# Low parts of the retention projection weights: a negated ScalarE copy plus an adding transfer in place of a VectorE subtraction

## The chip, the cores and the metric

The kernel runs on one core of one Trainium2 chip. The metric is the device time of one execution in microseconds (us). A core has TensorE (PE; its weight loads are listed as PEld), VectorE (DVE), ScalarE (ACT), GpSimd (POOL) and SyncE (SP), each with its own instruction stream in program order; streams meet only at semaphores. On-chip memory has 128 partitions; a tile "128x768" is 128 partitions by 768 elements.

## What is computed

Two decoder layers on 256 tokens of width 1024, in float32. Cut to what matters:

```python
for l in range(2):
    x = x + 0.5 * swiglu(rms_norm(x), ffn1_wg, ffn1_wu, ffn1_wd)   # hidden width 2816
    z = rms_norm(x) @ w_in[l]       # cut into rq rk rv rg mq mk mv ca cg
    mix = [retention(rq, rk, rv, rg), moba_attention(mq, mk, mv), conv_module(ca, cg)]
    x = x + concat(mix) @ w_out[l]
    x = x + 0.5 * swiglu(rms_norm(x), ffn2_wg, ffn2_wu, ffn2_wd)
return rms_norm(x, final_norm)
```

Retention uses four projections of width 384 (rq, rk, rv, rg), the attention three (mq, mk, mv), the convolution two of width 256.

## The kernel before

Every float32 weight matrix is multiplied as a sum of two parts: a high part `whi` (the weight rounded by a ScalarE copy to the type float32r) and a low part `wlo` (weight minus high part). The product of an activation and a weight is then high by high, high by low and low by high: `mm3` (lines 201 to 203), where the activations are the stationary operand, and `mm2w` (207, 208), where the weights are.

Weights come as a stream of 172 units. `stream_setup` lists them in the order of use; a unit of `w_in` (384 columns wide, half of the 1024 rows) is 128x1536, the others 128x2048. `fetch` issues one load on SP's queue into a `raw` tile, of which there are three (`RBUFS`); so a load waits until every reader of the unit three places earlier is done. `pump` makes one piece, half a unit: a ScalarE copy of `raw` into `whi` (line 145) and a VectorE subtraction into `wlo` (line 146). Ten pieces can be alive (`WBUFS`). `take` hands pieces to the matmuls, `free` returns a place, and `tick`, called between groups of matmuls, pumps at most one piece and advances the chains of work that were spawned (rotary embedding, attention, convolution, retention).

The PE instructions stand in the order in which the code issues them; the other engines' instructions are ordered by a planner that simulates the program at build time, except in short stretches that are marked as ordered.

The mixing stage (`mix`) takes the pieces in this order: mq and mk (8 pieces), the convolution's two gates (4), mv (4), then rq, rk, rv, rg (4 each), then the output projection (8). `chunk(w, t, ...)` runs the 24 matmuls of one projection for 128 tokens; its pieces are freed while the second half of the tokens runs. Around the retention weights these chains run:
- `rope`: a ScalarE copy out of PSUM (line 510), three GpSimd instructions on 128x96 (516 to 518), and four ticks later three PE transposes (line 505) and a ScalarE copy.
- `moba_group`: score matmuls (558), a VectorE maximum `nm` (562), ScalarE exponentials (569), PE transposes (576), ScalarE copies (578), matmuls with the values (588).
- `rot`: two VectorE products (528, 529), one GpSimd addition on 128x384 (530), transposes six ticks later.
- `conv`: 62 VectorE instructions of a depthwise convolution (693, 695), given a low rank by the planner.

In the profiled execution the pieces of rq to rg are, in each mixing stage, the 16 executions of line 145 that follow those of mv; in the first one they start at 224.12 us and end at 265.73.

Of the kernel before, what the change touches and what calls it, by code (L numbers as in the profile page):

```python
# [11 lines left out]
F32 = mybir.dt.float32  # L12
# [3 lines left out]
AF = mybir.ActivationFunctionType  # L16
OP = mybir.AluOpType
# [37 lines left out]
class Kernel:  # L55
# [38 lines left out]
    def stream_setup(self):  # L94
        a = self.a
        u = []
        for l in range(L):
            for f in (2 * l, None, 2 * l + 1):
                if f is None:
                    u += [(a["win"][l, 0, h], 1536) for h in range(2)]  # L100
                    u += [(a["win"][l, 1, h], 1536) for h in range(2)]
                    u += [(a["wcv"][l, i], 2048) for i in range(2)]
                    u += [(a["win"][l, i, h], 1536) for i in range(2, 7) for h in range(2)]
                    u += [(a["wout"][l, i], 2048) for i in range(4)]
                    continue
                u += [(a["wga"][f, i], 2048) for i in range(2)]
                for p in range(1, FT // 2):
                    u += [(a["wgb"][f, 2 * p - 2 + i], 2048) for i in range(2)]
                    if p > 1:
                        u.append((a["wd"][f, p - 2], 2048))  # L110
                u += [(a["wd"][f, i], 2048) for i in range((FT - TAIL) // 2, FT // 2)]
        self.units = u
        self.raws = []
        self.npieces = 0
        self.live = 0
        self.ready = deque()
# [13 lines left out]
    def pump(self):  # L130
        nc = self.nc
        u, i = divmod(self.npieces, 2)
        if u == len(self.units) or self.live == WBUFS:
            return False
        while len(self.raws) < min(u + RBUFS, len(self.units)):
            self.fetch()
        raw, w = self.raws[u]
        hi = self.wp.tile([P, 1024], F32R, tag="whi", bufs=WBUFS, name=self.name("whi"))[:, :w]
        lo = self.wp.tile([P, 1024], F32R, tag="wlo", bufs=WBUFS, name=self.name("wlo"))[:, :w]
        parts = 2 if u < 2 else 1  # L140
        p = w // parts
        for j in range(parts):
            c = slice(j * p, (j + 1) * p)
            src = raw[:, i * w + j * p:i * w + (j + 1) * p]
            nc.scalar.activation(hi[:, c], src, AF.Copy)  # L145
            nc.vector.tensor_tensor(lo[:, c], src, hi[:, c].bitcast(F32), op=OP.subtract)  # L146
        self.ready.append((hi, lo))
        self.npieces += 1
        self.live += 1
        return True  # L150
# [834 lines left out]
```

## Time and profile before

| | before |
|---|---|
| median of 3 runs, us | 1001.3 (999.83 to 1002.02) |
| the profiled execution: time, us | 1000.19 |
| its span, first to last instruction, us | 998.4 |
| granted TensorE clock (mean) | 0.998 |
| PE busy | 981.6 us (98%) |
| DVE busy | 685.5 us (69%) |
| ACT busy | 537.9 us (54%) |
| POOL busy | 64.1 us (6%) |
| DMA, mean | 181 GB/s |

The profile tells for each engine how long it was busy, and for an idle stretch which other instruction ended it. A PE that is busy 98% of the span has 16.8 us without work in all. The first mixing stage runs from about 205 to 312 us, the second from about 694 to 802.

### The profile page before, as it was taken

The numbers are of one execution on the slowest core, as the hardware profiler recorded it, in microseconds if no ns is written. First come the engines' busy times: TensorE is split into PE (matmuls) and PEld (weight loads), VectorE is DVE, ScalarE is ACT, GpSimd is POOL, SyncE is SP. The second block draws the span as 40 slices with busy tenths as digits, with TensorE's granted clock in tenths as the row PEclk, the third lists the DMA queues.
The fourth block names the chain that finished last, engine by engine and source line by source line (L and its number), as shares of the span: only waits on it lengthen the run. The fifth ranks groups of instructions, "written<-read, shape, count | busy, mean of one in ns | idle before, by whom it ended". The sixth has DMA issues, their size and how long they took to land.

```text
span 998.4 us, 13763 instructions
## 1 busy us (share of the span) xinstructions
PE 981.6 (98%) x5312; PEld 847.6 (85%) x5312; DVE 685.5 (69%) x1032; ACT 537.9 (54%) x904; POOL 64.1 (6%) x109
## 2 busy tenths in 40 slices
PE   6999999999999999999999999999999999999997
PEld 5888888898998888888888888888989888888885
DVE  6886565569976866666576656566699677666653
ACT  6755555366554755555465545454665456555542
POOL 1000000021141000000000000002100400000000
PEclk9999999999999999999999999999999999999999
DMA  8955554336441855555546555544545347555511
GB/s 309 347 194 201 175 204 156 142 122 214 170 170 64 302 204 172 201 177 199 181 173 218 179 193 186 188 150 139 186 143 197 138 148 253 175 204 174 205 44 43
DMA packets 28722, 180.69 MB, mean 181 GB/s; under 512 B 3440, under 2 KB 3824, under 8 KB 10480
## 3 DMA queue, kind: packets, MB, share of 16 engines
q1 hardware_dynamic: 27360, 176.07, 50.7%
q10 hardware_dynamic: 1296, 3.74, 1.0%
q8 instruction: 42, 0.69, 0.3%
q14 instruction: 24, 0.20, 0.1%
HBM read 178.74 MB, written 1.05 MB: 180 GB/s over the span
## 4 chain that ended last, share of the span: by engine, by line
PE 90%; DVE 6%; DMA 1%; ACT 1%; issue 1%; SPq 0%; POOL 0%; POOLq 0%; ACTq 0%; DVEq 0%
PE tr L207 15%; PE mm L207 15%; PE acc L451 8%; PE acc L448 8%; PE acc L447 8%; PE tr L208 7%; PE mm L208 7%; PE mm L201 4%; PE mm L202 4%; PE mm L203 4%; DVE wlo L146 3%; DVE ac L695 2%; PE acc L207 1%; PE tr L354 1%; PE acc L638 1%
## 5 line engine op out<-in xcount | busy, mean ns | idle before, releaser
L146 DVE TENSOR_TENSOR wlo<-raw,whi 128x1024 fp32r<-128x1024 f32 (+2 forms) x348 | 403.3, 1171 | 184.1 <-ACT whi L145 180.3
L145 ACT ACTIVATE whi<-raw 128x1024 fp32r<-128x1024 f32 (+2 forms) x348 | 348.6, 1013 | 229.0 <-PE acc L451 92.3
L207 PE MATMUL tr<-hT,whi 128*128 128x512 f32 x640 | 228.0, 397 | 0.2 <-DVE hfl L197 0.2
L207 PE MATMUL mm<-hT,whi 128*128 128x512 f32 x640 | 227.3, 396 | 0.0
L208 PE MATMUL mm<-hT,wlo 128*128 128x256 f32 x640 | 178.7, 279 | 0.0
L208 PE MATMUL tr<-hT,wlo 128*128 128x256 f32 x640 | 178.7, 279 | 0.0
L207 PEld LDWEIGHTS tr<-hT,whi 128*128 128x128 f32 x640 | 120.2, 188 | 29.2 <-PE mm L208 0.4
L207 PEld LDWEIGHTS mm<-hT,whi 128*128 128x128 f32 x640 | 120.2, 188 | 28.5
L447 PE MATMUL acc<-whi,hfh 128*128 128x512 f32 x352 | 139.2, 395 | 0.0
L448 PE MATMUL acc<-wlo,hfh 128*128 128x512 f32 x352 | 138.7, 394 | 0.0
L208 PEld LDWEIGHTS mm<-hT,wlo 128*128 128x128 f32 x640 | 120.6, 189 | 1.5
L208 PEld LDWEIGHTS tr<-hT,wlo 128*128 128x128 f32 x640 | 120.7, 189 | 0.0
L451 PE MATMUL acc<-whi,hfl 128*128 128x512 f32 x352 | 115.8, 396 | 0.0
L201 PE MATMUL mm<-whi,hT 128*128 128x384 f32 (+1 forms) x288 | 106.7, 371 | 0.7 <-ACT hT L196 0.7
L203 PE MATMUL mm<-whi,hT 128*128 128x384 f32 (+1 forms) x288 | 101.2, 351 | 0.0
L202 PE MATMUL mm<-wlo,hT 128*128 128x384 f32 (+1 forms) x288 | 101.1, 351 | 0.0
L447 PEld LDWEIGHTS acc<-whi,hfh 128*128 128x128 f32 x352 | 66.5, 189 | 15.1
L451 PEld LDWEIGHTS acc<-whi,hfl 128*128 128x128 f32 x352 | 66.3, 188 | 15.2
L448 PEld LDWEIGHTS acc<-wlo,hfh 128*128 128x128 f32 x352 | 66.3, 188 | 13.7
L433 ACT ACTIVATE s<-part 128x256 f32<-128x256 f32 x80 | 33.2, 414 | 79.2 <-DVE part L213 79.1
L213 DVE TENSOR_TENSOR part<-part,tr 128x256 f32<-128x256 f32 x80 | 33.6, 420 | 47.1 <-ACT part L212 47.1
L201 PEld LDWEIGHTS mm<-whi,hT 128*128 128x128 f32 x288 | 54.7, 190 | 5.5 <-issue 1.3
(151 smaller groups left out, 954.2 us busy)
## 6 DMA issues: line engine op xcount, KB each, us to landing
raw<-in_wgb SPq DMA_DIRECT2D x80, 1024.0 KB, 4.9
raw<-in_wd SPq DMA_DIRECT2D x44, 1024.0 KB, 4.9
raw<-in_win SPq DMA_DIRECT2D x28, 768.0 KB, 4.6
raw<-in_wout SPq DMA_DIRECT2D x8, 1024.0 KB, 4.8
raw<-in_wga SPq DMA_DIRECT2D x6, 1024.0 KB, 5.3
raw<-in_wcv SPq DMA_DIRECT2D x4, 1024.0 KB, 4.8
raw<-in_wga SPq DMA_DIRECT2D x8, 256.0 KB, 6.9
g<-in_fgain ACTq DMA_DIRECT2D x3, 512.0 KB, 3.5
```

The costliest lines, as they stand in the source:

```text
L145: nc.scalar.activation(hi[:, c], src, AF.Copy)
L146: nc.vector.tensor_tensor(lo[:, c], src, hi[:, c].bitcast(F32), op=OP.subtract)
L201: mm(out, ah, wh, start=start, stop=False)
L202: mm(out, ah, wl, start=False, stop=False)
L203: mm(out, al, wh, start=False, stop=stop)
L207: mm(out, wh, x, start=start, stop=False)
L208: mm(out[:, :S], wl, x[:, 0], start=False, stop=stop)
L213: self.nc.vector.tensor_tensor(v, lo, ps[:, :S], op=OP.add)
L433: nc.scalar.activation(s, v, AF.Silu)
L447: mm(ys[t][h], hi[:, ts], wh[:, n], start=first, stop=False)
L448: mm(ys[t][h], hi[:, ts], wl[:, n], start=False, stop=False)
L451: mm(ys[t][h], lo[:, ts], wh[:, n], start=False, stop=last)
```

## The change

For the eight units of rq, rk, rv and rg in each layer (units 41 to 48 and 127 to 134 of the stream, counted from 0), which make 32 of the 348 executions of line 146, the subtraction is replaced by two steps: ScalarE writes the negated weight, rounded, into `wlo`, and a transfer that GpSimd issues adds the raw weight to it in place. The sum is the same low part. All other pieces keep the subtraction.

```diff
     def stream_setup(self):
         a = self.a
         u = []
+        self.added = set()
...
                     u += [(a["wcv"][l, i], 2048) for i in range(2)]
+                    self.added |= {len(u) + i for i in range(2, 10)}
                     u += [(a["win"][l, i, h], 1536) for i in range(2, 7) for h in range(2)]
...
             nc.scalar.activation(hi[:, c], src, AF.Copy)
-            nc.vector.tensor_tensor(lo[:, c], src, hi[:, c].bitcast(F32), op=OP.subtract)
+            if u in self.added:
+                nc.scalar.activation(lo, src, AF.Copy, scale=-1.0)
+                nc.gpsimd.dma_start(lo, src, accum_op=OP.add)
+            else:
+                nc.vector.tensor_tensor(lo[:, c], src, hi[:, c].bitcast(F32), op=OP.subtract)
```

## Rows read from the trace of the kernel before

**Rows 1.** The page's first part: busy us (share of the span) xinstructions.
```profile
PE 981.6 (98%) x5312; PEld 847.6 (85%) x5312; DVE 685.5 (69%) x1032; ACT 537.9 (54%) x904; POOL 64.1 (6%) x109
```
**Rows 2.** Busy time by stretch: stretch, its length, each engine, PE clock, DMA share, GB/s.
```profile
0.00:205.00 205.00, 196.27 (x1012) 166.75 (x1013) 139.97 (x226) 114.10 (x191) 8.30 (x27) 1.00 0.60 210
...
220.00:290.00 70.00, 69.59 (x467) 65.92 (x466) 67.24 (x122) 41.12 (x77) 8.96 (x13) 1.00 0.50 173
...
710.00:780.00 70.00, 69.59 (x468) 65.97 (x466) 67.34 (x122) 41.57 (x78) 9.27 (x13) 1.00 0.50 172
802.00:998.40 196.40, 189.55 (x984) 160.41 (x984) 118.41 (x167) 98.69 (x163) 3.20 (x9) 0.99 0.46 158
```
**Rows 3.** Waits of PE, whole span: us in total, times, longest us.
```profile
PE tr L354 <- DVE xr L348: 8.5, 3, 8.1
PE acc L588 <- ACT q L578: 0.8, 2, 0.4
```
**Rows 4.** Groups of instructions by shape: lines 146 and 145, 768 wide.
```profile
L146 DVE TENSOR_TENSOR wlo<-raw,whi 128x768 fp32r<-128x768 f32 x56 | 52.1, 950 | 13.4 <-ACT whi L145 13.4
...
L145 ACT ACTIVATE whi<-raw 128x768 fp32r<-128x768 f32 x56 | 46.2, 845 | 20.9 <-PE mm L203 9.4 <-PE acc L451 3.7 <-PE mm L207 3.2
```
**Rows 5.** Timeline of ACT, first mixing stage: start us, us, instruction [idle before, releaser].
```profile
224.12 0.85 ACT L145 ACTIVATE whi<-raw 128x768 fp32r<-128x768 f32 x1 [0.19 <-PE mm L203]
...
225.91 0.47 ACT L510 ACTIVATE w<-mm 128x384 f32<-128x384 f32 x1
...
235.21 0.85 ACT L145 ACTIVATE whi<-raw 128x768 fp32r<-128x768 f32 x1 [0.51 <-PE mm L203]
...
238.44 0.37 ACT L569 ACTIVATE q<-acc,nm 128x128 f32<-128x128 f32 x1 [1.08 <-DVE nm L562]
...
240.41 0.22 ACT L569 ACTIVATION_READ_ACCUMULATOR q<-acc,nm 128x1 f32 x1
```
**Rows 6.** Timeline of POOL, first mixing stage.
```profile
204.59 0.99 POOL L516 TENSOR_TENSOR r<-w,pc 128x96 f32<-128x96 f32 x1 [1.82 <-ACT w L510]
...
210.31 0.40 POOL L516 TENSOR_TENSOR r<-w,pc 128x96 f32<-128x96 f32 x1 [2.05 <-ACT w L510]
...
226.47 0.80 POOL L516 TENSOR_TENSOR r<-w,pc 128x96 f32<-128x96 f32 x1 [14.95 <-ACT w L510]
...
227.75 0.40 POOL L518 TENSOR_TENSOR w<-r,r 128x96 f32<-128x96 f32 x1
...
231.02 0.46 POOL L518 TENSOR_TENSOR w<-r,r 128x96 f32<-128x96 f32 x1
```
**Rows 7.** Timeline of PE, first mixing stage.
```profile
229.13 0.49 PE L505 MATMUL tr<-ident,w 128*128 128x128 f32 x3
...
233.63 0.49 PE L505 MATMUL tr<-ident,w 128*128 128x128 f32 x3
...
239.56 0.33 PE L201 MATMUL mm<-whi,hT 128*128 128x384 f32 x1
...
240.61 0.49 PE L576 MATMUL tr<-ident,q 128*128 128x128 f32 x3
...
291.59 0.33 PE L203 MATMUL mm<-whi,hT 128*128 128x384 f32 x1
```
**Rows 8.** Timeline of SP: one load issue in the first mixing stage.
```profile
227.04 0.33 SPq L125 DMA_DIRECT2D raw<-in_win  x1
```
**Rows 9.** DMA issues (KB each, median us to landing); then all loads of raw.
```profile
raw<-in_win SPq DMA_DIRECT2D x28, 768.0 KB, 4.6
...
g<-in_fgain ACTq DMA_DIRECT2D x3, 512.0 KB, 3.5
...
DMA to landing us min/median/max: 4.1/4.9/7.7
```
**Rows 10.** Timeline of DVE, first mixing stage.
```profile
242.81 2.68 DVE L146 TENSOR_TENSOR wlo<-raw,whi 128x768 fp32r<-128x768 f32 x3
245.42 1.27 DVE L562 TENSOR_REDUCE nm<-acc 128x2 f32<-128x512 f32 x2
```

## The prediction

> **What bounds the kernel now.** I read the busy times first. PE works 981.6 of 998.4 us [rows 1]; the reader is to see that all other engines together can give back at most the 16.8 us in which PE has nothing to do. The table by stretch says where these are [rows 2]: 8.7 us before 205 us and 6.9 after 802, at the two ends of the program, where the change does nothing. In the two stretches in which the retention pieces are made, 220 to 290 and 710 to 780, PE is busy 69.59 of 70 us, while DVE is busy 67.24 and 67.34. So DVE is full there and yet PE hardly waits for it. The list of PE's waits agrees [rows 3]: 8.5 us for the norms at the ends, and 0.8 us, twice 0.4, for the attention's copies. The timelines of ACT, DVE, POOL, PE and SP then tell how much room each helper has before PE would wait. I use the first stage; the second repeats it 489.7 us later.
>
> **The change part by part.**
>
> *VectorE loses 32 subtractions* of 0.950 us [rows 4], 30.4 us, 15.2 in each stage. Of this PE can see only what it waits for now. One such place is known: three low parts at 242.81 keep the maximum `nm` back to 245.42 [rows 10], and the exponentials, copies and PE follow; that is the 0.41 us of PE per stage. Credit: at most 2 x 0.41 = 0.8 us. The rest of the 30.4 is worth nothing, because PE's order is fixed and PE is full.
>
> *ScalarE gains 32 copies.* A copy of the same shape takes 0.845 us [rows 4]; 27.0 us in all, 13.5 per stage, on top of 41.12 in 70 us [rows 2]: 78%. On average it fits. But an in-order engine is late in a burst: the first high part of rq begins at 224.12, the next copies follow PE's freeing closely, and the rope's copy out of PSUM (line 510) stands at 225.91 [rows 5]. Two negated copies fall before it if they rank before it: 2 x 0.845 = 1.7 us. Behind that copy hang three POOL instructions, which end at 227.75 + 0.40 = 228.15 [rows 6], and the transposes on PE at 229.13 [rows 7]: 0.98 us of room. The second rope has 233.63 - 231.48 = 2.15 us [rows 6, 7]. A cost of 1.7 - 0.98 = 0.7 us per stage, or none if the planner puts line 510 first.
>
> *POOL gains 32 transfer issues*, each waiting for its negated copy; queued behind it are the rope's instructions (516 to 518), which the PE transposes need, and later the rotation's additions (530), which have room of many us. No row shows an issue on POOL. The nearest price is SP's, 0.33 us [rows 8]; from above I take about 1 us, an estimate at the length of POOL's own small instructions (0.40 to 0.99) [rows 6]. One issue ahead of the rope: 0.33 taken (below nothing it cannot be, POOL has no work less), 1.0 for the range, per stage.
>
> POOL's rows show another thing: line 516 takes 0.99 us at 204.59 and 0.40 at 210.31 [rows 6], the first beside two-input VectorE work, the second not. The Trainium skill's page "SBUF — State Buffer", section "Who interferes with whom", says that a VectorE instruction with two SBUF inputs contends with GpSimd's reads, and a two-port mode locks out the generation of descriptors for GpSimd's transfers. The rows agree with the first; no row here shows the second. By it an issue would take 2.5 times its price, about 0.5 us more per stage.
>
> *The transfer* moves 128x768 floats, 384 KB, inside SBUF and adds. No row shows one. Nearest are a 512 KB load, 3.5 us to landing, and the 768 KB loads, 4.6; loads of raw reach 7.7 at most [rows 9]. It reads two operands and shares the DMA engines, half busy in this stretch [rows 2], so I take 4.6, with 3.5 and 10 (an estimate: the 7.7, and its excess over 4.9 once more, rounded down) as ends. Who waits? First PE: the low part of rq's first piece is ready by 226.2 us or so and PE takes the piece at 239.56 [rows 7]: 13 us of room, against 0.845 + 0.33 + 4.6 - 0.95 = 4.8 us of delay. Hidden; without that cover, each us would count. Second, `raw`: a unit now stays occupied until the transfer has read it, so the load three places on starts later. This is the first rival.
>
> *Sum for the forecast:* per stage +0.7 (ScalarE ahead of the rope) +0.33 (issue) -0.41 (the wait that goes) = +0.6; two stages: +1.2 us. The profiled execution took 1000.19 us, 998.4 of span and 1.8 around it; 1000.2 + 1.2 = 1001.4. The median of the three runs is 1.1 us above the profiled execution; I carry this over: **1002.5 us**. For this case alone I give 1000.5 to 1003.3: from the credit without the cost up to twice the cost. The sign of a difference under 0.2%, 2 us, can't be told by measuring this kernel; this is the bound of my three chances.
>
> **Rivals.**
>
> *A: the raw buffers turn late and ScalarE stands in line for them (slower).* The load issued at 227.04 [rows 8] is of the unit whose first high part is made at 235.21 [rows 5]. It lands after 4.6, at 231.6, so 3.6 us early. It waits for the last reader of the second rq piece. After the change this reader ends later by two negated copies (1.7), an issue (0.33) and a landing (4.6), less the subtraction (0.95): 5.7 us. The high part then comes 2.1 us late. If it stands ahead of the exponentials in ScalarE's order, as now, it and its negated copy (0.845) push them, and ScalarE's idle time of 1.08 before them [rows 5] absorbs part: 2.1 + 0.85 - 1.08 = 1.9 us. The exponentials end at 240.41 + 0.22 = 240.63 and PE's transposes start at 240.61 [rows 5, 7]: no room at all, so PE stands for 1.9 us. Per stage with the forecast's +0.6: 2.5; both: +5, **1006.3 us** at the median. It decides from a landing of about 2.7 us on (where the lateness of 1.9 is used up), and only if the planner leaves the high part ahead of the exponentials; a planner that expects the transfer to be slow puts them first, and nothing happens. With a landing of 7.7 it would be +5.6 per stage, 1012.5. For it speaks that no room stands at 240.6; against it, that VectorE's maxima come earlier without the subtractions. Chance 0.37.
>
> The Trainium skill's page "DMA: Bandwidth & Descriptors", section "Anatomy of one DMA — SWDGE (gpsimd) path", fits a GpSimd transfer's time as 2.0 us plus bytes over 436 GB/s. That makes 2.9 us here, an estimate by that page, and nearly no loss in rival A. No row here shows such a transfer; the 512 KB load's 3.5 us is a little above what the fit gives it, 3.2.
>
> *B: the transfers are so slow that the stream of pieces itself is late (much slower).* A raw place would turn in 4.6 (load) + 4 x 0.845 (copies) + 1 (issue) + landing; PE takes the eight units of rq to rg between 239.56 and 291.92 [rows 7], one in 6.5 us, so three places may take 19.5. So the landing must pass some 10.5 us; at 15 the stream loses 4.5/3 = 1.5 us per unit, 12 us per stage less the 13 us of room. Only at 20 us does it cost, 25 - 13 = 12 us per stage, 1025 us. Chance 0.06.
>
> *C: faster.* All of PE's waiting in the two stretches is 0.82 us [rows 2], and the forecast's costs don't arise: 999.4 for the profiled execution, 1000.4 at the median, under 0.2%. To pass 2 us, the altered order of the planner would have to help at the ends of the program, where the retention pieces aren't made. Chance of that 0.06, at about 998.5.
>
> **How the numbers follow.** Forecast 0.51 (with C's small gain, which lies within 0.2%), A 0.37, B 0.06, C beyond 0.2% 0.06. The forecast is the likeliest: 1002.5. Part of A ends under 2 us (the landing near its threshold, or in one stage alone), and about as much of the forecast, with dear issues, ends above it. So faster 0.06, same 0.51, slower 0.43. The range leaves out B, C and the dearest part of A: 1000.2 to 1009.
>
> **What would show it.** In the profile after, the stretch 220 to 290 should show DVE some 15 us lower and ACT 13 us higher, with PE near 69 of 70 us. Line 145's waits should show more time under the loads of w_in if A is true, and PE's waits should name the exponentials' transposes (576) or copies (578) with some us. If the forecast is right, PE's new waits name line 505 and stay at about 1 us per stage. A wait of line 202 for the transfer would be B. The forecast is wrong if PE's waits in these stretches pass 2 us, and the sum is wrong in kind if a difference comes from outside of them. The landing times of the new transfers settle their price at once.

## The result and the profile after

| | before | after |
|---|---|---|
| median, us | 1000.85 (6 runs, 999.83 to 1002.02) | 1038.78 (6 runs, 1035.96 to 1043.94) |
| after over before, 95% interval | | 1.038 (1.0358 to 1.0402) |
| the profiled execution: time; span, us | 1000.19; 998.4 | 1038.73; 1037.0 |
| granted TensorE clock (mean) | 0.998 | 0.983 |

The changed kernel is 38 us slower; the forecast was 1002.5 and its range ended at 1009. From the subtraction on, line numbers after are those of before plus 6: 146 is now 152, the rope's ScalarE copy 516, its GpSimd instructions 522 to 524, its transposes 511. The high copy 145 is now 147; the negated copy is 149, the transfer 150.

The first part of the page after (busy us, share, instructions), beside [rows 1]:

```profile
PE 992.1 (96%) x5312; PEld 856.6 (83%) x5312; DVE 653.6 (63%) x1000; ACT 559.4 (54%) x936; POOL 110.4 (11%) x141
```

PE is idle for 1037.0 - 992.1 = 44.9 us in place of 16.8: 28.1 more. It is also busy for 10.5 us more with the same 5312 instructions. The two make the 38.6 us between the spans. PE's waits over the whole span of after (us in total, times, longest), beside [rows 3]:

```profile
PE tr L511 <- POOL w L524: 20.8, 2, 10.4
PE tr L360 <- DVE xr L354: 8.7, 3, 8.2
PE acc L629 <- DVE q L636: 6.4, 2, 3.9
PE tr L582 <- ACT q L584: 1.2, 2, 0.6
```

The norms' wait (360) is as before. New are two waits of 10.4 us for the rope's last GpSimd instruction, one per mixing stage, and two of up to 3.9 at the retention scores (629), late in each stage: their PSUM tile comes free with a VectorE product (636). The table by stretch of after (stretch, length, PE, PEld, DVE, ACT, POOL, PE clock, DMA share, GB/s), beside [rows 2]:

```profile
0.00:205.00 205.00, 195.95 (x1008) 166.10 (x1009) 139.51 (x226) 113.35 (x190) 7.44 (x26) 1.00 0.60 210
220.00:290.00 70.00, 58.99 (x361) 55.80 (x360) 41.69 (x93) 44.66 (x84) 30.54 (x26) 0.93 0.84 206
230.00:240.00 10.00, 0.00 (x0) 0.00 (x0) 9.10 (x23) 3.91 (x6) 9.92 (x3) 0.73 0.54 141
240.00:250.00 10.00, 9.80 (x52) 9.18 (x53) 0.32 (x1) 3.43 (x7) 5.42 (x9) 0.76 0.89 152
710.00:780.00 70.00, 58.99 (x357) 54.54 (x356) 45.98 (x98) 48.05 (x91) 32.04 (x31) 0.93 0.71 187
```

Ahead of the stage nothing has changed. From 230 to 240 us PE does nothing at all, and POOL is busy for the whole stretch with three instructions. The timeline of POOL there (start, us, instruction), beside [rows 6]:

```profile
227.98 0.87 POOL L150 DMA_DIRECT2D wlo<-raw  x1 [0.35 <-ACT wlo L149]
228.56 10.78 POOL L522 TENSOR_TENSOR r<-w,pc 128x96 f32<-128x96 f32 x1
239.31 0.37 POOL L523 TENSOR_TENSOR r<-w,pn 128x96 f32<-128x96 f32 x1
239.76 0.39 POOL L524 TENSOR_TENSOR w<-r,r 128x96 f32<-128x96 f32 x1
...
737.20 10.81 POOL L522 TENSOR_TENSOR r<-w,pc 128x96 f32<-128x96 f32 x1
```

The product of line 522 took 0.80 us at this place before [rows 6] and takes 10.78 now. Its like in the second stage takes 10.81. DVE's timeline of after shows what stands beside it:

```profile
226.34 12.75 DVE L701 SCALAR_TENSOR_TENSOR ac<-u,vec,ac 128x256 f32<-128x256 f32 x32
```

These are convolution instructions of low rank, each with two inputs in SBUF (u and ac): 32 without a break, to 239.09. The GpSimd instruction ends at 239.34, a quarter of a microsecond later. In the kernel before the subtractions stood between them (DVE, before):

```profile
227.74 0.68 DVE L695 SCALAR_TENSOR_TENSOR ac<-u,vec,ac 128x256 f32<-128x256 f32 x1
228.34 1.81 DVE L146 TENSOR_TENSOR wlo<-raw,whi 128x768 fp32r<-128x768 f32 x2
230.08 1.68 DVE L695 SCALAR_TENSOR_TENSOR ac<-u,vec,ac 128x256 f32<-128x256 f32 x3
231.69 1.81 DVE L146 TENSOR_TENSOR wlo<-raw,whi 128x768 fp32r<-128x768 f32 x2
```

PE in after, behind the wait, beside [rows 7]:

```profile
240.20 0.90 PE L511 MATMUL tr<-ident,w 128*128 128x128 f32 x3 [10.42 <-POOL w L524]
...
243.14 0.52 PE L208 MATMUL mm<-wlo,hT 128*128 128x384 f32 x1
...
245.34 0.33 PE L207 MATMUL mm<-whi,hT 128*128 128x384 f32 x1
```

For some 4.5 us after the wait the same matmul takes 0.52 in place of 0.33 us, and the granted clock of the stretch is 0.76. The same happens behind the waits at 629, and outside of these waits and of what follows them the clock is near 1.00, as before. That is where the 10.5 us of busy time come from: a wait of PE can be paid a second time. How much, its length doesn't tell: after_raw_free, below, keeps both waits of 10.4 us, and PE is busy there for 984.6 us, only 3.0 more than before.

### The profile page after: what moved, and what is told of

Read it like the earlier page. It is cut to its first block, busy times and chain, and to the rows that moved or that the text cites. A ratio compares the mean times of both kernels' runs of the same rounds, so it can differ in the third digit from the quotient of the medians.

```text
span 1037.0 us, 13851 instructions
## 1 busy us (share of the span) xinstructions
PE 992.1 (96%) x5312; PEld 856.6 (83%) x5312; DVE 653.6 (63%) x1000; ACT 559.4 (54%) x936; POOL 110.4 (11%) x141
## 3 DMA queue, kind: packets, MB, share of 16 engines
q10 hardware_dynamic: 1296, 3.74, 1.0%
## 4 chain that ended last, share of the span: by engine, by line
PE 89%; DMA 3%; ACT 3%; POOL 2%; DVE 1%; issue 1%; SPq 0%; POOLq 0%; ACTq 0%
PE tr L213 14%; PE mm L213 14%; PE acc L457 8%; PE acc L453 8%; PE acc L454 8%; PE mm L214 7%; PE tr L214 7%; PE mm L207 4%; PE mm L208 4%; PE mm L209 4%; POOL r L522 2%; DMA wlo<-raw 2%; PE acc L213 1%; ACT whi L147 1%; PE tr L360 1%; DMA raw<-in_wout 1%
## 5 line engine op out<-in xcount | busy, mean ns | idle before, releaser
L152 DVE TENSOR_TENSOR wlo<-raw,whi 128x1024 fp32r<-128x1024 f32 (+2 forms) x316 | 374.5, 1195 | 201.0 <-ACT whi L147 196.3
L207 PE MATMUL mm<-whi,hT 128*128 128x384 f32 (+1 forms) x288 | 109.2, 379 | 0.8 <-ACT hT L202 0.8
L208 PE MATMUL mm<-wlo,hT 128*128 128x384 f32 (+1 forms) x288 | 103.5, 359 | 0.0
L209 PE MATMUL mm<-whi,hT 128*128 128x384 f32 (+1 forms) x288 | 103.5, 359 | 0.0
L347 POOL TENSOR_SCALAR e<-ss 128x1 f32<-128x1 f32 x14 | 3.7, 261 | 689.5 <-ACT sq L344 689.5
```

What stands on the lines that cost most here:

```text
L207: mm(out, ah, wh, start=start, stop=False)
L208: mm(out, ah, wl, start=False, stop=False)
L209: mm(out, al, wh, start=False, stop=stop)
```

## The experiments

Two theories of the 10 us stood at the start. Theory 1: the change takes the subtractions out of DVE, what is left is one unbroken run of two-input instructions, and a GpSimd instruction that reads SBUF can't finish beside it. Theory 2: the new transfers, issued by GpSimd, hold it up. The diffs are against the changed kernel.

| label | rope on | negated copy | transfer reads | us |
|---|---|---|---|---|
| (before) | GpSimd | none | none | 1000.9 |
| relief_alone | GpSimd | none | none | 1023.6 |
| relief_breaks | GpSimd | none | none | 1021.0 |
| relief_rope_vec | VectorE | none | none | 999.7 |
| after_no_transfer | GpSimd | ScalarE | none | 1024.6 |
| rope_vec_neg_only | VectorE | ScalarE | none | 1006.2 |
| after_raw_free | GpSimd | ScalarE | device memory | 1026.1 |
| rope_vec_hbm | VectorE | ScalarE | device memory | 1006.4 |
| (after) | GpSimd | ScalarE | raw | 1038.8 |
| rope_on_vector | VectorE | ScalarE | raw | 1029.4 |
| conv_after_rope | GpSimd | ScalarE | raw | 1033.7 |
| vector_neg_add | GpSimd | VectorE | raw | 1016.9 |

The times of before and after and of relief_rope_vec, after_raw_free and after_no_transfer are medians of several executions; the other experiments are one execution each, and before alone spread over 2 to 3 us. Without a transfer the low part of the 32 pieces isn't made: in the relief rows the high part stands in for it, in after_no_transfer and rope_vec_neg_only the negated copy. They show time and not the layers' result.

**relief_alone.** The 32 subtractions are taken away, with nothing in their place; the matmuls read the high part twice.

```diff
+        lo = hi if u in self.added else self.wp.tile([P, 1024], F32R, tag="wlo", bufs=WBUFS, name=self.name("wlo"))[:, :w]
...
-                nc.scalar.activation(lo, src, AF.Copy, scale=-1.0)
-                nc.gpsimd.dma_start(lo, src, accum_op=OP.add)
+                lo = hi
```

> For the 32 pieces the subtraction is taken away and nothing is put in its place: the high part stands in for the low part too, so the low parts of rq, rk, rv and rg are left out of the result. No negated copy, no transfer. Theory 1 (VectorE, without the subtractions, runs some 32 convolution instructions with two inputs in one unbroken run, and GpSimd's rope instruction, which needs the same path to memory, gets none until the run ends): GpSimd's first rope instruction of the second token block takes about 10 us in each mixing stage, PE waits 8 to 10 us for it twice, and with the lower TensorE clock behind each wait the time is 1020 to 1030 us. Theory 2 (the adding transfers that GpSimd issued just before it hold it up): the instruction takes 0.4 to 1 us, and the time is 999 to 1001 us.

1023.6 us. There is no transfer and no added copy, and yet (POOL, then DVE, then PE's waits):

```profile
227.40 10.79 POOL L521 TENSOR_TENSOR r<-w,pc 128x96 f32<-128x96 f32 x1 [14.94 <-ACT w L515]
```
```profile
226.78 11.17 DVE L700 SCALAR_TENSOR_TENSOR ac<-u,vec,ac 128x256 f32<-128x256 f32 x28
```
```profile
PE tr L510 <- POOL w L523: 17.7, 2, 8.8
```

The run ends at 237.95, the GpSimd instruction at 238.19. Theory 2 falls, and taking the subtractions from DVE costs 22.7 us by itself. The hold of GpSimd until the run ends is called the lock-out from here on.

**vector_neg_add.** The negation goes back to VectorE, so that 32 instructions of the subtraction's shape stand where it stood; the transfers stay.

```diff
-                nc.scalar.activation(lo, src, AF.Copy, scale=-1.0)
+                nc.vector.scalar_tensor_tensor(lo, src, 0.0, hi.bitcast(F32), op0=OP.mult, op1=OP.subtract)
```

> The changed kernel, but the negated high part is written by VectorE (an instruction with two inputs, raw and high part, in the place of the old subtraction) and the transfer adds raw to it as in the changed kernel. VectorE's work is again about that of the kernel before; the 32 transfers stay. Theory 1: GpSimd's rope instructions take 0.4 to 2 us, PE's waits for them vanish or are under 2 us a stage; what remains is the late turn of the raw buffers, 3 to 5 us a stage with its clock: 1005 to 1015 us. Theory 2: the 10 us instruction stays, about 1035 us.

1016.9 us, a little above the 1005 to 1015 expected. The wait for POOL falls from 10.4 to 1.9 us a stage:

```profile
PE tr L511 <- POOL w L524: 3.8, 2, 1.9
PE mm L207 <- DVE w L535: 3.7, 2, 1.9
```

With the run broken the first rope's GpSimd instructions take 1.63, 2.13 and 0.46 us. There are still 16 us left without any copy on ScalarE; ScalarE's waits for loads of raw (11.6 us for the output projection's, 6.4 for the input projection's) point to something else that the transfers do.

**conv_after_rope.** The convolution can't begin before the second rope is done: its padding is made from the rope's result. A second edit shortens the pause behind the convolution's products from 14 ticks to 6, as they begin later.

```diff
-CONV_WAIT = 14
+CONV_WAIT = 6
...
+                if mark == "mk" and t == 1:
+                    nc.gpsimd.tensor_scalar(u[:, :, 0:pad], z[:, :2 * pad].rearrange("p (c j) -> p c j", c=2), 0.0, None, op0=OP.mult)
+                    self.spawn(conv())
...
-            nc.gpsimd.memset(u[:, :, 0:pad], 0.0)
...
-            self.spawn(conv())
```

> The changed kernel, but the convolution's products on VectorE can't begin before the second rope is done on GpSimd: its zero padding is made out of that rope's result, and the chain of the convolution is started there; PE's order of work is the same. Transfers and negated copies stay. Theory 1: the rope instructions take 0.4 to 2 us and PE waits under 3 us for them in each stage; 1005 to 1018 us. Theory 2: the 10 us instruction stays, 1035 us or more.

The instruction behaved as theory 1 had it, the time did not: 1033.7 us. POOL, then PE's waits:

```profile
228.04 0.70 POOL L522 TENSOR_TENSOR r<-w,pc 128x96 f32<-128x96 f32 x1
```
```profile
PE tr L585 <- ACT q L578: 6.5, 2, 3.5
PE acc L632 <- DVE q L639: 5.7, 2, 3.4
```

The 10 us are gone, and other waits have taken their place: the attention's transposes (585 here) stand for ScalarE's exponentials, which is the place of rival A, and the retention scores (632 here) for VectorE. With two edits in it, this run shows what becomes of the GpSimd instruction, and not what the wait alone is worth.

**rope_on_vector.** The three rope instructions go to VectorE, so that none of them can be held up on GpSimd; all else is the changed kernel.

```diff
-                nc.gpsimd.tensor_tensor(t1, zr, cb, op=OP.mult)
-                nc.gpsimd.tensor_tensor(t2.rearrange("p h (i f) -> p h i f", i=2), sw, sb, op=OP.mult)
-                nc.gpsimd.tensor_tensor(zr, t1, t2, op=OP.add)
+                nc.vector.tensor_tensor(t1, zr, cb, op=OP.mult)
+                nc.vector.tensor_tensor(t2.rearrange("p h (i f) -> p h i f", i=2), sw, sb, op=OP.mult)
+                nc.vector.tensor_tensor(zr, t1, t2, op=OP.add)
```

> The changed kernel, but the three rope instructions run on VectorE and not on GpSimd; transfers and negated copies stay. By both theories PE's 10.4 us wait in each stage goes. What is left measures the other part, the late turn of the raw buffers (PE's wait of 3.2 us on average for the retention scores, and the clock behind it): about 1008 to 1016 us. If the time stays over 1025, GpSimd's slow instruction was not what PE lacked.

A miss again: 1029.4 us. ScalarE, PE, and PE's waits:

```profile
243.34 0.84 ACT L149 ACTIVATE wlo<-raw 128x768 fp32r<-128x768 f32 x1 [6.46 <-DMA raw<-in_win]
...
246.23 0.37 ACT L575 ACTIVATE q<-acc,nm 128x128 f32<-128x128 f32 x1
```
```profile
246.74 1.18 PE L582 MATMUL tr<-ident,q 128*128 128x128 f32 x3 [3.74 <-ACT q L575]
```
```profile
PE tr L582 <- ACT q L575: 6.1, 2, 3.7
PE acc L629 <- DVE q L636: 4.7, 2, 2.4
```

ScalarE stands 6.46 us in line for a unit of raw whose load was issued late, and the exponentials stand behind it: rival A, step by step. By the expectation a time over 1025 us would mean that GpSimd's slow instruction was not what PE lacked; that holds only while the raw tiles are held, for relief_rope_vec, below, takes 23.9 us off relief_alone by this same edit. In the changed kernel this wait can't be seen at 240 us, since there PE itself comes 10 us late and the load has landed by then.

**relief_breaks.** relief_alone, with a tiny one-input instruction on 128x8 after every eight convolution instructions; in the order that the planner gives, nine stand between two of them.

```diff
+                        if j % 4 == 2:
+                            tiny = self.small.tile([P, 8], F32, tag="tiny", name=self.name("tiny"))
+                            nc.vector.tensor_scalar(tiny, ac[1][:, :8], 1.0, None, op0=OP.mult)
```

> As the kernel with the subtractions taken away and nothing in their place (low parts of rq, rk, rv and rg left out: the high part stands in), but into the convolution's run on VectorE a tiny instruction with one input (128x8) is put after every eight or so of the 128x256 ones. Theory 1, in the form that GpSimd gets in wherever VectorE's instruction needs only one input from memory: GpSimd's rope instruction takes at most one stretch of eight, 0.8 to 4 us, PE's wait for it falls from 8.8 to under 3 us a stage: 1000 to 1008 us. Theory 1, in the form that VectorE must stand idle first: it stays at about 10 us and 1023 us.

1021.0 us, neither of the two times expected, and PE's wait falls only from 8.8 to 6.6 a stage. POOL and DVE show why:

```profile
228.58 1.66 POOL L521 TENSOR_TENSOR r<-w,pc 128x96 f32<-128x96 f32 x1 [14.97 <-ACT w L515]
230.20 3.86 POOL L522 TENSOR_TENSOR r<-w,pn 128x96 f32<-128x96 f32 x1
234.14 3.75 POOL L523 TENSOR_TENSOR w<-r,r 128x96 f32<-128x96 f32 x1
```
```profile
229.90 0.37 DVE L703 TENSOR_SCALAR tiny<-ac 128x8 f32<-128x8 f32 x1
230.18 3.64 DVE L700 SCALAR_TENSOR_TENSOR ac<-u,vec,ac 128x256 f32<-128x256 f32 x9
233.74 0.35 DVE L703 TENSOR_SCALAR tiny<-ac 128x8 f32<-128x8 f32 x1
```

Each GpSimd instruction ends with the next break, at 230.24, 234.06 and 237.89, and each break lets one pass. The rope has three.

**relief_rope_vec.** The edits of relief_alone and of rope_on_vector together: DVE's relief without the lock-out.

> The subtractions of the 32 pieces are taken away with nothing in their place (low parts of rq, rk, rv and rg left out: the high part stands in), and the rope's three instructions run on VectorE instead of GpSimd. This is what the relief of VectorE alone is worth once nobody is locked out. The sum of the prediction: PE's 0.82 us of waits go at most, 999 to 1001 us, no gain that can be measured. If the relief were worth something, below 998.

999.7 us, a ratio of 0.9989 (0.998 to 0.9999). DVE's 30 us are worth about 1 us when nothing else goes wrong, and between this run and relief_alone lies only the engine of the rope: 23.9 us.

**rope_vec_neg_only** is rope_on_vector with the negated copies and without the transfers (the first line of this diff alone); in **rope_vec_hbm** the transfers are there, but read the weights from device memory, so that raw is free after ScalarE (both lines).

```diff
-                nc.gpsimd.dma_start(lo, src, accum_op=OP.add)
+                nc.gpsimd.dma_start(lo, self.units[u][0][:, i * w:(i + 1) * w], accum_op=OP.add)
```

> The changed kernel with the rope on VectorE, and without the transfer: the low parts of rq, rk, rv and rg stay the negated copies, the adding is left out. It prices the 32 negated copies on ScalarE alone. The prediction's term: 0.7 us per stage or none, 1000 to 1003 us. If ScalarE's load itself makes the attention's copies late, 1005 to 1010.

> The changed kernel with the rope on VectorE, and the transfers read the weights to add from device memory and not from the raw buffer, which is then free after ScalarE's copies. Transfers, negated copies and their issues all stay. If the 28 us that remain with the rope on VectorE come from the raw buffers held by the transfers (rival A of the prediction), PE's waits for the exponentials (3 us a stage) and for the retention scores (2.4 us) go: 1000 to 1006 us. If they come from the transfers themselves (late low parts, DMA traffic), it stays near 1029 us.

1006.2 and 1006.4 us. The copies cost 6.5 us. ScalarE in relief_rope_vec, then in rope_vec_neg_only, then PE in the latter:

```profile
230.08 0.49 ACT L515 ACTIVATE w<-mm 128x384 f32<-128x384 f32 x1 [0.65 <-PE mm L208]
```
```profile
234.59 0.47 ACT L515 ACTIVATE w<-mm 128x384 f32<-128x384 f32 x1
```
```profile
236.63 0.52 PE L510 MATMUL tr<-ident,w 128*128 128x128 f32 x3 [1.95 <-DVE w L523]
```

The planner puts eight copies, four high and four negated, between the first rope's copy out of PSUM and the second's, which comes 4.5 us later, and PE waits 1.95 us for that rope in each stage. Another 0.6 us a stage are PE's wait for the attention's copies (583); the last 1.4 of the 6.5 us aren't placed. The transfers by themselves cost nothing that can be told, even though those from device memory land late (DMA issues of rope_vec_hbm; KB, median us to landing):

```profile
wlo<-in_win POOLq DMA_DIRECT2D x32, 384.0 KB, 13.3
```

Between rope_vec_hbm and rope_on_vector lies only what the transfer reads, so that raw is held until it has landed: 1029.4 - 1006.4 = 23 us. Loads land late beside the transfers in both (up to 10.0 and 9.7 us in the first stage, 6.7 before), but with raw free early they are also issued early. Of the spans' 22.9, 9.6 are PE's idle time and 13.3 its busy time at a lower clock (0.985 against 0.998).

**after_raw_free** and **after_no_transfer** make the same two edits with the rope on GpSimd: the transfer from device memory, and no transfer.

> The changed kernel as it is, except that each adding transfer reads the weights from device memory instead of from raw, so that raw is free after the second ScalarE copy; the rope stays on GpSimd. If lock-out and held raw buffers add up, this saves the 23 us that separate rope_on_vector (1029.4) from rope_vec_hbm (1006.4): 1016. If they overlap, because PE's 10 us wait for the rope gives the loads time to arrive, little is saved: the floor of 999.7, the lock-out's 23.9 (relief_alone 1023.6 less 999.7) and the copies' 6.5 give 1030, and PE's wait for the rope stays at 9 to 10 us per stage while the wait for the query maxima at the end of the stage goes.

> The changed kernel without the transfers (the low parts stay the negated weights); rope on GpSimd, negated copies on ScalarE. No descriptor work on GpSimd at all. If the transfers' issues have a part in the wait for the rope, it falls clearly under 9 us per stage and the time under 1025. If the lock-out by VectorE's unbroken convolution alone makes it, the wait stays at 9 to 10 us per stage, and the time is that of the run with the weights read from device memory, within 3 us: about 1030.

1026.1 (ratio 1.0253, 1.0234 to 1.0272) and 1024.6 us (1.0232, 1.0215 to 1.0248). PE's first waits in after_raw_free, and in after_no_transfer:

```profile
PE tr L511 <- POOL w L524: 20.8, 2, 10.4
PE tr L360 <- DVE xr L354: 9.8, 3, 9.3
```
```profile
PE tr L510 <- POOL w L523: 20.0, 2, 10.0
```

The wait for the rope doesn't need the transfers: 10.0 us without them. (By the time alone, just under 1025, the expectation would have given their issues a part; the wait says no.) The wait at the retention scores (629) is gone with the held raw tiles, and 12.7 us with it: neither the 1016 of a plain sum nor the 1030 of a full overlap. The copies, 6.5 us alone, cost 1 us behind the lock-out (relief_alone to after_no_transfer).

So the 38 us are: about 23 for the lock-out, 1 for the copies behind it, 1.4 for the transfers and 12.7 for the held raw tiles, taken in this order; the 1 and the 1.4 are too small to be told from nothing. In another order the shares differ, as the causes cover each other: with the rope on VectorE the copies are 6.5 and the held tiles 23. Of the changed versions that compute all of the result none is under 1006 us; before stays the fastest.

## Why the prediction was wrong

**The failed step** is "the rest of the 30.4 is worth nothing, because PE's order is fixed and PE is full". As a gain it was right: relief_rope_vec gives 1.1 us where the step had 0.8 at most. But it asked only what PE gains from a shorter DVE, and not what stands next to what in DVE when the subtractions are gone. The convolution's 62 instructions had been named as of low rank; without the subtractions nothing is ahead of them, and 32 fall together (28 in relief_alone) exactly where the rope needs GpSimd. That costs 22.7 us (relief_alone); the step's own cover, the rope's 0.98 us of room, had been worked out a paragraph later and was set against ScalarE and an issue alone.

**The row was read and mis-sized.** The 0.99 against 0.40 us of [rows 6] is a rope product beside DVE; its factor of 2.5 was applied to the new issue (0.5 us a stage) and not to the products for which the row stands. And 2.5 was no upper bound, not even for its own place, where four subtractions stand on DVE: in the changed kernel that product takes 1.00 us in the first stage and 3.28 in the second, where it ends 0.25 us behind the last of them (POOL, after):

```profile
205.20 1.00 POOL L522 TENSOR_TENSOR r<-w,pc 128x96 f32<-128x96 f32 x1 [1.81 <-ACT w L516]
...
713.84 3.28 POOL L522 TENSOR_TENSOR r<-w,pc 128x96 f32<-128x96 f32 x1 [1.79 <-ACT w L516]
```

Beside the unbroken convolution the factor is 10.78 over 0.40, 27. The Trainium skill's page "SBUF — State Buffer", section "Who interferes with whom", has the direction (two SBUF inputs contend with GpSimd's reads), and the traces agree; it gives no size for this pair, and 10.78 us is the size here. Its other half, the locked-out descriptors, doesn't show: the issue at 227.98 lies inside the run and takes 0.87 us.

**ScalarE's copies.** Two of them stand ahead of the first rope copy, as the prediction had it, and it begins at 227.57 in place of 225.91, 1.66 us later. The whole stage begins 0.5 us later in this trace (rq's first high part at 224.62), so that 1.2 us are left for the 1.7 worked out. The term was too small all the same, 1.4 for 6.5 us: the second rope was dismissed by its 2.15 us of room, without counting the copies that would stand ahead of it. 4.5 us late less that room makes 2.35, and 1.95 were measured.

**The transfer.** The DMA issues of after, beside [rows 9]:

```profile
wlo<-raw POOLq DMA_DIRECT2D x32, 384.0 KB, 6.3
raw<-in_wout SPq DMA_DIRECT2D x8, 1024.0 KB, 7.1
```

In the median 6.3 us to landing where 4.6 was taken, and an issue of 0.87 where 0.33 was taken: both inside their bounds, the nearest row too cheap for each. The Trainium skill's page "DMA: Bandwidth & Descriptors", section "Anatomy of one DMA — SWDGE (gpsimd) path", made it 2.9 us by its fit; the trace is more than twice that. That PE doesn't wait for the piece itself was right: at 13.3 us still nothing (rope_vec_hbm), and rival B didn't come.

**Rival A** was right in kind and place, and under-priced. By its sum a landing of 6.6 us instead of 4.6 makes the wait 1.9 + 2.0 = 3.9 us; rope_on_vector shows 3.74, but that is luck. The load was issued at 233.58 there in place of 227.04, 6.5 us later for the 5.7 worked out, and it took 9.7 us to land, not 4.6; before, this very load took 6.7 and had 1.5 us to spare, not 3.6. So ScalarE's copies came 8.1 us late (243.34 for 235.21) and the exponentials 7.8, not the 2 of the sum. Against that stand 1.7 us of room where the prediction had "no room at all", since PE's first transpose needs the first exponential alone (it starts 0.5 us behind it in rope_on_vector, 2.2 before), and the 2.4 us that PE was late itself when it came there.

The rival stopped at the retention pieces. But the held tiles also delay the loads of the output projection: in the changed kernel they begin at 274.94 in place of 254.18. ScalarE waits for one of them, VectorE's two subtractions stand behind it, and behind these the product of the retention scores, for which PE stands at 629 (ACT, then DVE, after):

```profile
294.60 2.00 ACT L147 ACTIVATE whi<-raw 128x1024 fp32r<-128x1024 f32 x2 [4.08 <-DMA raw<-in_wout]
```
```profile
295.69 2.36 DVE L152 TENSOR_TENSOR wlo<-raw,whi 128x1024 fp32r<-128x1024 f32 x2 [4.11 <-ACT whi L147]
297.96 2.21 DVE L636 TENSOR_TENSOR q<-acc,decay 128x384 f32<-128x384 f32 x4
```

That is 3.9 us of PE in after and 2.4 in rope_on_vector. And the rival counted each wait once: in rope_on_vector 9.6 us of added idle time go with 13.3 us of slower matmuls. 23 us, not 5. In the changed kernel its own wait, at the exponentials, doesn't show, because the lock-out's wait of 10 us lies ahead of it and gives the load time to land. But the lock-out also holds the raw tiles longer, as the transfers stand behind the rope in GpSimd's order: the third negated copy ends at 229.51, and its transfer is issued at 240.27 (POOL, after). So the 12.7 us put down to the held tiles contain a part of the lock-out that no run separates.

```profile
240.27 3.57 POOL L150 DMA_DIRECT2D wlo<-raw  x4
```

**What the prediction said would show that it is wrong** did: PE's waits in these stretches pass 2 us by far. PE in 220 to 290 has 58.99 us in place of the 69 named, and the new wait is at the rope's transposes as the forecast had it, at 10.4 in place of about 1 us. DVE fell by 25.6 us there, not 15, and ACT rose by 3.5, not 13, since the lost 10 us push work out of the stretch. Rival A's sign, high copies that wait for loads, shows too, but for w_out: 13.4 us, none before, and 0.3 for w_in. PE's waits at 511, 629 and 582 make 28.4 us, all in or right behind the mixing stages, against 28.1 us of added idle time: next to nothing comes from elsewhere. The range reached into rival A, without its dearest part, and had no case of a GpSimd instruction held for 10 us. A slip without weight: the 1003.3 called twice the cost is about the cost without the credit; twice the cost makes 1004.6.

## What to carry to other kernels

When work leaves an engine that isn't the bound, look at what closes up in its place: a run of low-rank instructions that nothing interrupts any more can hold up another engine far more than the work removed ever did. A row that shows two engines disturbing each other is a price for that occasion alone; beside a longer run the price can be the length of the run. And a transfer that reads a buffer in place of an engine lengthens that buffer's life by its landing time, and PE can pay for a wait twice, the second time in matmuls at a lower clock.

## What the runs showed of the hardware

- A GpSimd product on 128x96 with 0.4 us of work takes 10.78 us beside 32 back-to-back VectorE instructions with two SBUF inputs, 10.79 beside 28, and ends 0.25 us after the run.
- A one-input VectorE instruction of 0.35 us between two runs of nine lets one GpSimd instruction pass; the next then waits for the following break, 3.8 us later (relief_breaks).
- What lets GpSimd through in the kernel before isn't settled. The second rope's instructions (POOL, before; the last is the 231.02 of [rows 6]) pass there beside a subtraction and the run of three convolution instructions at 230.08, all with two SBUF inputs. These three take 0.56 us each (1.68 over 3), while the 32 of after take 0.40 (12.75 over 32): there the two engines share. In the changed kernel the rope product beside the same four subtractions does the one in the first stage (1.00 us, the subtractions 4.50) and the other in the second (3.28 us, the subtractions 4.09), at starts 1.08 and 1.06 us behind theirs. So neither the shapes nor the length of the run settles it, and what does was not tried; beside the unbroken convolution it was the wait in both stages of all four kernels that have it with the rope on GpSimd (after, relief_alone, after_raw_free, after_no_transfer).

```profile
229.90 0.52 POOL L516 TENSOR_TENSOR r<-w,pc 128x96 f32<-128x96 f32 x1 [1.75 <-ACT w L510]
230.38 0.57 POOL L517 TENSOR_TENSOR r<-w,pn 128x96 f32<-128x96 f32 x1
```

- Right behind four transfer issues a rope product on GpSimd takes 1.73 us with VectorE idle (242.53, after), and 0.39 at the same place without transfers (after_no_transfer). PE didn't wait for it.
- A load of 768 KB issued among the transfers took 9.7 us to land (rope_on_vector, 233.58), and 6.7 at this place before.
- Behind a wait of 10 us, in which PE did nothing, the granted clock was 0.76 in the next 10 us, with matmuls at 0.52 in place of 0.33 us for 4.5 us; the two levels are 1.2 and 2.4 GHz. Behind the wait of 3.85 us at 294.7 the matmuls of line 208 took 0.52 us as well; behind the wait of 1.95 us in rope_vec_neg_only none did.
